# A modulation row summed on TensorE in two bursts, the row before it released later

## The chip, the core and the metric

The kernel runs on one core of a Trainium2 chip. The metric is the device time of one execution in microseconds (us), as the median of several runs. Five engines work side by side: TensorE (PE, matrix products; its weight loads are listed as PEld), VectorE (DVE), ScalarE (ACT), GpSimd (POOL) and SyncE (SP, which here only issues transfers). Each engine takes its own instructions in the order in which the program wrote them. An engine waits when an operand is not there, or when a buffer that it is to write is still being read.

## What is computed

Two transformer layers in a row over 256 positions of width 1024, in float32. The change lies in the second layer, which begins with six modulation rows:

```
mod = silu(c) @ mod_w + mod_b          # c: one row of 1024; mod_w: 1024 x 6144
shift1, scale1, gate1, shift2, scale2, gate2 = split(mod, 6)
h = rms_norm(x) * (1 + scale1) + shift1
(sc_b, sc_c, sc_x, q, k, v, z, xbc, dt_raw, gl_a, gl_b, gl_c) = split_columns(h @ w_in)
y_a = short_conv_mixer(sc_b, sc_c, sc_x) @ w_sc_out
y_b = stick_breaking_attention(q, k, v) @ w_sb_out
y_c = mamba2_mixer(z, xbc, dt_raw) @ w_ssm_out
merged = sigmoid(gl_a) * y_a + sigmoid(gl_b) * y_b + sigmoid(gl_c) * y_c
x = x + gate1 * rms_norm(merged @ w_o)
h2 = rms_norm(x) * (1 + scale2) + shift2      # then a gated FFN, gate2, residual
```

The rows are numbered g = 0 to 5 in the order shift1, scale1, gate1, shift2, scale2, gate2. Rows 3 and 4 (shift2, scale2) are read only after `w_o`.

## The kernel before

**Projections.** Every float32 product is made of three passes in a rounded format: each weight tile of 128 x 1024 is loaded by SP into `wst` (4 buffers), rounded by ACT into `wh` (L202), and DVE forms the rest `wl` (L203). PE then multiplies `x3h` with `wh`, `x3h` with `wl` and `x3l` with `wh` (L377, L379, L381, in rows of four matmuls of 256 columns). A *unit* is two such weight tiles, 12 rows of four matmuls, into one PSUM bank. SP can load a tile only when L203 has freed a `wst` buffer.

**The mixer of the second layer.** Its units come in the order that `mix2_order` gives: `qk0`, `qk1`, `xbc1`, `xbc0`, `xbc2` (the state-space channels, in three pairs), `sc1`, `sc0`, `sc2` (the short convolution), and then the gates `gl` of three branches, each with an output projection that writes `mg`. An `xbc` unit is followed by a convolution over the positions: ACT makes the first tap (L660), DVE the other three (L664), ACT a tanh, and a last DVE instruction sets the flag `xbc0`, `xbc1` or `xbc2`. Units, scores and bursts draw their PSUM banks from one pool of four, in turn: a unit cannot begin before the unit four places ahead of it in that pool has been read.

**Work beside it.** Whatever is not a projection is written as a generator in the list `chains`. `beside()` gives every chain one step; it is called twice for each weight tile, so after every three rows of four matmuls. `pause(name)` waits as many steps as the table `LAG` says, `need(flag)` waits until a flag is set, and `hold(1)` and `held` count PSUM banks. Two large chains run here: `stick_steps`, the attention (scores `z3`; ACT L1689 to L1691; DVE L1693, L1695; PE L1700 to L1704; DVE L1708; ACT L1710, L1712; PE L1719) and `ssm_steps`, the state-space scan (DVE L1622, L1623; ACT L1624; DVE L1634; PE L1671 to L1673).

**Modulation rows.** `mod_steps` makes one row after the other. A row needs 8 tiles `raw` of 128 x 1024 (512 KB each), which POOL loads ahead into 4 buffers. There are two ways to sum a row:

- for rows in `BY_SUMS`, DVE multiplies each tile by its scalar and adds it into `macc` (L1404, then L1406), one tile a step; 3 idle steps later four matmuls against ones (L1394) sum over the partitions;
- for the others, PE does it all: one step is a *burst* of 16 matmuls (L1394), four tiles times four column groups of 32 PE columns, into one bank.

After each sum DVE adds the bank to the row (L1396); POOL then writes the finished row out (L1425) and reads it back onto all partitions (L1426). Before the change, rows 0, 1 and 4 are in `BY_SUMS`. The first two and a half rows are done before the mixer; the second burst of row 3 and all of row 4 (12 steps) are the chain `mods_beside`, whose steps are separated by the pauses `mod` (2) and `mod2` (7). The chain sets the flag `mods`, for which the kernel waits ahead of `w_o`. Row 5 is done later, beside `w_o` and the FFN.

Of the kernel before, what the change touches and what calls it, by code (L numbers as in the profile page):

```python
# [19 lines left out]
KT = 8  # L20
# [9 lines left out]
for _n, _w in (("mlcw", 32), ("mlcb", 8), ("fcw", 132), ("fcb", 44), ("sccw", 6), ("ssmcw", 24),  # L30
# [33 lines left out]
WST = 4  # L64
WSP = 6

BY_SUMS = (0, 1, 4)

IDLE = 3

# [62 lines left out]
def block_pair(ctx, tc, a, out):  # L133
# [203 lines left out]
    chains, holders, heldA = [], [], [0]  # L337
# [9 lines left out]
    def need(*keys):  # L347
        while not flags.issuperset(keys):
            yield
# [110 lines left out]
    def drain(gen, n=None):  # L460
        if n is None:
            for _ in gen:
                pass
        else:
            for _ in range(n):
                next(gen, None)
# [258 lines left out]
    def pause(name, d=2):  # L725
        for _ in range(LAG[name]):
            yield


    held = [0]  # L730

    def hold(n):
        while held[0] + n > 4:
            yield
        held[0] += n
# [645 lines left out]
    def mod_steps():  # L1381
# [3 lines left out]
        for g in range(6):  # L1385
# [11 lines left out]

            if g in BY_SUMS:

# [32 lines left out]
    def mod_step(n=1):  # L1432
        drain(steps, n)
# [292 lines left out]

    def mods_beside(n):
        for i in range(n):
            mod_step()
            yield from pause("mod" if i < KT else "mod2")  # L1730
        flags.add("mods")

    chains.append(mods_beside(KT + IDLE + 2))

    def unit2(name, srcs, *stages):
        unit(name, srcs, xb, *stages, wide=False)
# [289 lines left out]
```

## Time and profile before

| | |
|---|---|
| median of 3 runs | 853.41 us (846.42 to 855.21) |
| the profiled execution | 853.56 us, of which the span from first to last instruction is 851.6 us |
| PE busy | 822.2 us (97%) |
| DVE busy | 601.4 us (71%) |
| ACT busy | 424.6 us (50%) |
| mixer of the second layer | from 452 to about 620 us |

PE is the engine that bounds the kernel: outside its first microseconds it rarely waits. So the time is read from where PE waits, from the clock that it is granted, and from what is put into its queue.

### The profile page before, as it was taken

The page shows a single profiled execution, that of the slowest core. Times are in us where ns is not written, and L with a number is a line of the kernel's source. Part 1 is how long each engine was busy: PE and PEld are TensorE (multiplying, and loading weights), DVE is VectorE, ACT ScalarE, POOL GpSimd, SP SyncE. Part 2 cuts the span into 40 slices and gives each one's busy share as a digit, 9 for nine tenths or more (in the row PEclk, how much of TensorE's full clock was granted, in tenths as well). Part 3 has the DMA queues.
Part 4 walks back from the last instruction along what each step waited for, and adds up shares of the span by engine and source line. Part 5 has one row for each costly group of instructions (what it writes and reads, how often), then busy time and mean ns, then how long its engine had stood idle before and what let it go on. Part 6 is the DMA issues. An engine that isn't in the chain of part 4 may idle for free.

```text
span 851.6 us, 14309 instructions
## 1 busy us (share of the span) xinstructions
PE 822.2 (97%) x5628; PEld 744.7 (87%) x5628; DVE 601.4 (71%) x1001; ACT 424.6 (50%) x633; POOL 64.6 (8%) x112
## 2 busy tenths in 40 slices
PE   6999999999999999999989999999999999999996
PEld 6999887998789998999769887999987799999994
DVE  4698688765748899887775987577579575554434
ACT  5655654455437567555343556454454464444421
POOL 1000200100010001000121210003110000000000
PEclk9999999999999999999999989999999999999999
DMA  7854774473445898886479964446666287556601
GB/s 263 311 162 139 259 249 152 136 255 99 150 148 178 283 325 269 332 266 210 138 286 383 347 228 149 144 142 193 184 222 252 78 257 249 188 183 188 190 33 49
DMA packets 50866, 176.03 MB, mean 207 GB/s; under 512 B 5900, under 2 KB 7088, under 8 KB 50800
## 3 DMA queue, kind: packets, MB, share of 16 engines
q1 hardware_dynamic: 40352, 138.64, 48.8%
q0 software_dynamic: 10448, 36.48, 12.5%
q8 instruction: 44, 0.72, 0.3%
q14 instruction: 22, 0.18, 0.1%
HBM read 174.02 MB, written 1.09 MB: 206 GB/s over the span
## 4 chain that ended last, share of the span: by engine, by line
PE 65%; DVE 9%; DMA 4%; ACT 3%; issue 2%; POOL 0%; DVEq 0%; ACTq 0%
PE pb L377 12%; PE pb L379 12%; PE pb L381 12%; PE pa L387 6%; PE pa L389 6%; PE pa L388 6%; PE pa L1248 3%; DVE wl L203 3%; ACT wh L202 1%; DMA wst<-in_w_xbc 1%; PE pa L381 1%; PE pa L379 1%; PE pa L377 1%; DMA wst<-in_w_sc 1%; PE pb L1180 1%
## 5 line engine op out<-in xcount | busy, mean ns | idle before, releaser
L203 DVE TENSOR_TENSOR wl<-wst,wh 128x1024 fp32r<-128x1024 f32 (+3 forms) x257 | 311.6, 1224 | 154.7 <-ACT wh L202 153.7
L202 ACT CAST wh<-wst 128x1024 fp32r<-128x1024 f32 (+3 forms) x257 | 263.8, 1037 | 242.8 <-PE pb L381 97.5
L387 PE MATMUL pa<-wh,hh 128*128 128x512 f32 x176 | 69.2, 393 | 0.7 <-ACT hh L202 0.7
L388 PE MATMUL pa<-wl,hh 128*128 128x512 f32 x176 | 69.3, 394 | 0.4 <-DVE wl L203 0.4
L389 PE MATMUL pa<-wh,hl 128*128 128x512 f32 x176 | 69.2, 393 | 0.0
L377 PE MATMUL pb<-x3h,wh 128*128 128x256 f32 x320 | 53.0, 288 | 1.9 <-DVE cv L664 1.9
L381 PE MATMUL pb<-x3l,wh 128*128 128x256 f32 x320 | 51.8, 285 | 0.0
L379 PE MATMUL pb<-x3h,wl 128*128 128x256 f32 x320 | 51.8, 284 | 0.0
L664 DVE SCALAR_TENSOR_TENSOR cv<-pb,sm,cv 128x255 f32<-128x255 f32 (+2 forms) x106 | 43.5, 474 | 11.6 <-ACT cv L660 11.6
L377 PEld LDWEIGHTS pb<-x3h,wh 128*128 128x128 f32 x320 | 44.7, 195 | 2.9 <-ACT lk L1691 2.1
L377 PE MATMUL pb<-x2h,wh 128*128 128x256 f32 x288 | 46.2, 282 | 0.0
L379 PE MATMUL pb<-x2h,wl 128*128 128x256 f32 x288 | 46.0, 282 | 0.0
L377 PE MATMUL pb<-x4h,wh 128*128 128x256 f32 x288 | 46.0, 282 | 0.0
L379 PE MATMUL pb<-x4h,wl 128*128 128x256 f32 x288 | 46.0, 282 | 0.0
L381 PE MATMUL pb<-x4l,wh 128*128 128x256 f32 x288 | 46.0, 282 | 0.0
L381 PE MATMUL pb<-x2l,wh 128*128 128x256 f32 x288 | 45.9, 282 | 0.0
L381 PEld LDWEIGHTS pb<-x3l,wh 128*128 128x128 f32 x320 | 44.6, 194 | 0.0
L379 PEld LDWEIGHTS pb<-x3h,wl 128*128 128x128 f32 x320 | 44.5, 193 | 0.0
L209 POOL DMA_DIRECT2D raw<-in_mod_w x48 | 25.3, 531 | 250.9 <-DVE macc L1406 97.0
L377 PEld LDWEIGHTS pb<-x2h,wh 128*128 128x128 f32 x288 | 39.7, 190 | 1.3 <-ACT wh L202 0.4
L377 PEld LDWEIGHTS pb<-x4h,wh 128*128 128x128 f32 x288 | 39.9, 190 | 0.7
L387 PEld LDWEIGHTS pa<-wh,hh 128*128 128x128 f32 x176 | 33.1, 188 | 7.8 <-ACT hh L202 1.1
(433 smaller groups left out, 1637.6 us busy)
## 6 DMA issues: line engine op xcount, KB each, us to landing
raw<-in_mod_w POOLq DMA_DIRECT2D x48, 512.0 KB, 6.7
wst<-in_ffn_up SPq DMA_DIRECT2D x44, 512.0 KB, 5.1
wst<-in_ffn_in SPq DMA_DIRECT2D x44, 512.0 KB, 4.2
wst<-in_w_gl SPq DMA_DIRECT2D x24, 512.0 KB, 3.7
wst<-in_ffn_down SPq DMA_DIRECT2D x22, 512.0 KB, 4.9
wst<-in_ffn_out SPq DMA_DIRECT2D x22, 512.0 KB, 3.6
wst<-in_w_qk SPq DMA_DIRECT2D x12, 512.0 KB, 6.7
wst<-in_xk SPq DMA_DIRECT2D x8, 512.0 KB, 4.0
```

Of the source, the lines that this page charges most:

```text
L202: A.copy(xh, src)
L203: V.tensor_tensor(xl, src, xh.bitcast(F32), ALU.subtract)
L209: (queue or nc.sync).dma_start(st[:, :n].rearrange("p (a b) -> p a b", a=src.shape[1]), src)
L377: T.matmul(dst, wh[:, k - k0, c0:c0 + P], xh[:, k, t0:t1], start=(k == ks[0]), stop=False)
L379: T.matmul(dst, wl[:, k - k0, c0:c0 + P], xh[:, k, t0:t1], start=False, stop=False)
L381: T.matmul(dst, wh[:, k - k0, c0:c0 + P], xl[:, k, t0:t1], start=False, stop=(k == ks[-1]))
L387: T.matmul(dst[:, c0:c1], xh[:, k, tsl], wh[:, kw, c0:c1], start=first, stop=False)
L388: T.matmul(dst[:, c0:c1], xh[:, k, tsl], wl[:, kw, c0:c1], start=False, stop=False)
L389: T.matmul(dst[:, c0:c1], xl[:, k, tsl], wh[:, kw, c0:c1], start=False, stop=last)
L664: V.scalar_tensor_tensor(dst[:, j:S], ps[:, 0:S - j], taps[K - 1 - j], dst[:, j:S], ALU.mult, ALU.add)
L1180: T.matmul(pl[:, tt * S:(tt + 1) * S], qx[:, 2 * h + e, tt * P:(tt + 1) * P], kx[:, 2 * h + e, :], start=(e == 0), stop=(e == 1))
L1248: T.matmul(pt, x_[:, 2 * i + kw, tsl], w_[:, kw, :], start=(i + n + kw == 0), stop=(i + n + kw == 6))
```

## The change

Row 4 leaves `BY_SUMS`, so it is summed by PE in two bursts. `mods_beside` has now three steps: the second burst of row 3, and the two of row 4. None of them is made until the flag `xbc0` is set (the second pair of state-space channels to be convolved), and 16 steps lie between one and the next.

```diff
-    "ml.4": 0, "ml.5": 1, "ml.s0": 4, "ml.s1": 7, "ml.s2": 9, "ml.s3": 4, "mod": 2, "mod2": 7, "no.0": 0, "no.1": 0, "no.2": 1,
+    "ml.4": 0, "ml.5": 1, "ml.s0": 4, "ml.s1": 7, "ml.s2": 9, "ml.s3": 4, "mod2": 16, "no.0": 0, "no.1": 0, "no.2": 1,
...
-BY_SUMS = (0, 1, 4)
+BY_SUMS = (0, 1)
...
     def mods_beside(n):
         for i in range(n):
+            yield from need("xbc0")
+            yield from hold(1)
             mod_step()
-            yield from pause("mod" if i < KT else "mod2")
+            held[0] -= 1
+            yield from pause("mod2")
         flags.add("mods")

-    chains.append(mods_beside(KT + IDLE + 2))
+    chains.append(mods_beside(3))
```

Three places show what moves. The first is DVE between the projections `qk` and the convolution of the first state-space pair (`xbc1`, whose taps are the three rows L664). Before:

```order
L203 TENSOR_TENSOR wl_5090<-wst_4933,wh_5089 128x1024
L1406 SCALAR_TENSOR_TENSOR macc_4949<-raw_4951,cs,macc_4949 128x1024
L203 TENSOR_TENSOR wl_5124<-wst_4989,wh_5123 128x1024
L1406 SCALAR_TENSOR_TENSOR macc_4949<-raw_5005,cs,macc_4949 128x1024
L203 TENSOR_TENSOR wl_5171<-wst_5023,wh_5170 128x1024
L1406 SCALAR_TENSOR_TENSOR macc_4949<-raw_5038,cs,macc_4949 128x1024
L664 SCALAR_TENSOR_TENSOR cv_5058<-pb_5060,sm,cv_5058 128x255 x2
L664 SCALAR_TENSOR_TENSOR cv_5058<-pb_5060,sm,cv_5058 128x254 x2
L664 SCALAR_TENSOR_TENSOR cv_5058<-pb_5060,sm,cv_5058 128x253 x2
```

The same place with the change:

```order
L203 TENSOR_TENSOR wl_5045<-wst_4903,wh_5044 128x1024
L203 TENSOR_TENSOR wl_5076<-wst_4953,wh_5075 128x1024
L203 TENSOR_TENSOR wl_5120<-wst_4984,wh_5119 128x1024
L664 SCALAR_TENSOR_TENSOR cv_5016<-pb_5018,sm,cv_5016 128x255 x2
L664 SCALAR_TENSOR_TENSOR cv_5016<-pb_5018,sm,cv_5016 128x254 x2
L664 SCALAR_TENSOR_TENSOR cv_5016<-pb_5018,sm,cv_5016 128x253 x2
```

All eight instructions on `macc` are gone from DVE, and with them the transfers of `raw` that each of them let go.

The second place is PE between the end of the attention's second score product (L1704) and the first outputs of the scan (L1671, which read `ar`). Before:

```order
L1703 MATMUL pa_5540<-qb,kb 128x128
L1704 MATMUL pa_5540<-lk_5586,ntri 128x128
L1394 MATMUL pb_5665<-macc_4949,triu 32x256 x4
L1671 MATMUL pa_5676<-xdt,ar_5638 128x64
L1672 MATMUL pa_5676<-xdt,ar_5638 128x64
```

With the change:

```order
L1703 MATMUL pa_5513<-qb,kb 128x128
L1704 MATMUL pa_5513<-lk_5559,ntri 128x128
L1394 MATMUL pb_5635<-raw_5383,cs 32x256 x4
L1394 MATMUL pb_5635<-raw_5385,cs 32x256 x4
L1394 MATMUL pb_5635<-raw_5387,cs 32x256 x4
L1394 MATMUL pb_5635<-raw_5389,cs 32x256 x4
L1671 MATMUL pa_5666<-xdt,ar_5611 128x64
L1672 MATMUL pa_5666<-xdt,ar_5611 128x64
```

The four matmuls that closed row 4 before are replaced at this very place by its first burst of 16. The row's second burst stands later, within the third `gl` unit; row 3's second burst has moved from the middle of `qk0` to the middle of `sc0`.

The third place is DVE at the same moment: L1708 masks the attention's scores, L1634 makes the `ar` that L1671 reads, L1396 empties the burst's bank. Before:

```order
L1623 SCALAR_TENSOR_TENSOR ar_5642<-aq_5276,acs,maskn 128x128
L1708 TENSOR_TENSOR att_5660<-pa_5540,maskn 128x2x128 x2
L1634 TENSOR_TENSOR ar_5638<-gm_5636,ar_5638 128x384
L1634 TENSOR_TENSOR ar_5642<-gm_5636,ar_5642 128x384
L1396 TENSOR_TENSOR brow_4947<-pb_5665,brow_4947 128x256
```

With the change:

```order
L1623 SCALAR_TENSOR_TENSOR ar_5615<-aq_5219,acs,maskn 128x128
L1396 TENSOR_TENSOR brow_5633<-pb_5635,brow_5633 128x256
L1708 TENSOR_TENSOR att_5661<-pa_5513,maskn 128x2x128 x2
L1634 TENSOR_TENSOR ar_5611<-gm_5609,ar_5611 128x384
L1634 TENSOR_TENSOR ar_5615<-gm_5609,ar_5615 128x384
```

L1396, which reads what the burst leaves, now stands ahead of L1708 and of both L1634.

## Rows read from the trace of the kernel before

**Rows 1.** PE's waits, 452 to 610 us: total us, times, longest.

```profile
PE pa L1700 <- DVE lk L1693: 2.0, 2, 1.1
PE pb L377 <- DVE cv L664: 1.9, 1, 1.9
PE pa L1671 <- DVE ar L1634: 0.7, 1, 0.7
```

**Rows 2.** Timeline of PE: start us, us, engine, line, operation, count [idle before <-releaser].

```profile
487.38 0.71 PE L377 MATMUL pb<-x3h,wh 128*128 128x256 f32 x4 [1.89 <-DVE cv L664]
...
491.42 0.70 PE L1700 MATMUL pa<-qb,kb 64*128 64x256 f32 x2 [0.92 <-DVE lk L1693]
...
493.72 1.12 PE L1700 MATMUL pa<-qb,kb 64*128 64x256 f32 x2
...
497.51 1.20 PE L377 MATMUL pb<-x3h,wh 128*128 128x256 f32 x4
```

**Rows 3.** Stretches of 4 us: PE busy (count), granted clock, DMA share, GB/s.

```profile
484.00:488.00 4.00, 2.11 (x18) 1.00 1.03 409
...
492.00:496.00 4.00, 4.00 (x15) 0.73 0.79 262
496.00:500.00 4.00, 4.00 (x17) 0.50 0.59 184
500.00:504.00 4.00, 4.00 (x32) 0.91 0.73 247
```

**Rows 4.** Timeline of ACT and DVE, 478 to 492 us.

```profile
478.82 1.05 ACT L202 CAST wh<-wst 128x1024 fp32r<-128x1024 f32 x1 [6.28 <-DMA wst<-in_w_sc]
...
481.40 1.05 ACT L202 CAST wh<-wst 128x1024 fp32r<-128x1024 f32 x1 [1.53 <-DMA wst<-in_w_sc]
482.36 1.02 ACT L660 ACTIVATE cv<-pb,sm 128x256 f32<-128x256 f32 x2
...
484.82 2.42 DVE L664 SCALAR_TENSOR_TENSOR cv<-pb,sm,cv 128x255 f32<-128x255 f32 x6
...
490.41 0.95 DVE L1693 SCALAR_TENSOR_TENSOR lk<-pa,lk 128x768 f32<-128x768 f32 x1
```

**Rows 5.** DVE's groups on `macc`, 466 to 490 us: busy us, mean ns of one.

```profile
L1406 DVE SCALAR_TENSOR_TENSOR macc<-raw,cs,macc 128x1024 f32<-128x1024 f32 x7 | 8.9, 1278 | 0.0
...
L1404 DVE TENSOR_SCALAR macc<-raw,cs 128x1024 f32<-128x1024 f32 x1 | 0.8, 751 | 0.0
```

**Rows 6.** DMA issues, 440 to 540 us: count, size, median us to landing.

```profile
raw<-in_mod_w POOLq DMA_DIRECT2D x16, 512.0 KB, 8.0
wst<-in_w_gl SPq DMA_DIRECT2D x10, 512.0 KB, 3.7
wst<-in_w_sc SPq DMA_DIRECT2D x8, 512.0 KB, 7.4
```

**Rows 7.** Timeline of PE: a burst in `qk0`, and what follows it.

```profile
453.65 1.93 PE L1394 MATMUL pb<-raw,cs 128*32 128x256 f32 x32
455.52 0.74 PE L377 MATMUL pb<-x3h,wh 128*128 128x256 f32 x4
```

**Rows 8.** Timeline of PE and DVE at the end of row 4.

```profile
528.75 0.64 PE L1394 MATMUL pb<-macc,triu 128*32 128x256 f32 x8
528.86 0.75 DVE L1708 TENSOR_TENSOR att<-pa,maskn 128x256 f32<-128x256 f32 x2 [1.53 <-PE pa L1704]
529.53 1.02 DVE L1634 TENSOR_TENSOR ar<-gm,ar 128x384 f32<-128x384 f32 x2
...
530.13 0.43 PE L1671 MATMUL pa<-xdt,ar 128*128 128x64 f32 x2 [0.74 <-DVE ar L1634]
```

**Rows 9.** Timeline at a burst of row 5, for which DVE waits.

```profile
665.21 1.93 PE L1394 MATMUL pb<-raw,cs 128*32 128x256 f32 x32
...
667.21 0.42 DVE L1396 TENSOR_TENSOR brow<-pb,brow 128x256 f32<-128x256 f32 x1 [0.58 <-PE pb L1394]
```

**Rows 10.** Timeline of PE ahead of the mixer: a long single wait.

```profile
439.87 1.29 PE L480 MATMUL pb<-ident,h__729_4638 128*128 128x128 f32 x8 [2.49 <-DVE h__729_4638 L1472]
```

## The prediction

> **What bounds the kernel now.** I read three views in this order: PE's waits in the mixer, the clock granted there, and what DVE, ACT and the DMA queues do ahead of the waits. PE is the bound: from 452 to 610 us it waits for only 4.6 us in all [rows 1]. So a change pays here only through those waits and the clock, and costs whatever PE work it adds.
>
> Two of the waits stand close together: 1.89 us before unit `sc1`, whose bank DVE has not yet emptied of `xbc1`, and 0.92 us before the attention's second scores [rows 2]. Shortly after them the granted clock falls to half, 1.2 instead of 2.4 GHz: 0.73, 0.50 and 0.91 of full speed over three stretches of 4 us in which PE is busy throughout [rows 3]. That costs 4 x (0.27 + 0.50 + 0.09) = 3.4 us. The place loses 1.89 + 0.92 + 3.4 = 6.2 us altogether. PE had worked without a break until the first of the two waits, so I take the fall to be their result.
>
> Why do they arise? The convolution of `xbc1` on DVE (L664) begins at 484.82 and ends 2.42 us later, just when PE can go on; its first tap on ACT (L660) came at 482.36, behind two roundings of weights that had waited 6.28 and 1.53 us for their transfers [rows 4]. The transfers are late because DMA is full: a share of 1.03 at 409 GB/s [rows 3], with sixteen tiles `raw` landing after 8.0 us and `w_sc` after 7.4 us, where `w_gl`, mostly later, needs 3.7 us [rows 6]. DVE meanwhile spends 8.9 + 0.8 = 9.7 us on `macc` [rows 5].
>
> **The change part by part.**
>
> *DVE's sums leave.* Eight instructions, 9.7 us of DVE [rows 5], stood between the weights' L203 and the convolution. With them go the transfers of `raw` that they released one at a time; and since row 3's second burst now waits for `xbc0`, no new `raw` is loaded until then. If `w_sc` lands like `w_gl`, 3.7 us earlier [rows 6], ACT's two waits (7.8 us) shrink by about half or more: I estimate that L660 comes 4 to 5 us earlier, and DVE, with no `macc` ahead, makes L664 at about 478 to 479. PE reaches `sc1` at 485.49 (487.38 less the wait) in this trace, and 1.87 us sooner without the burst in `qk0`, at 483.6. DVE is then done with a margin of some 2 us. The wait at L1700 depends on L1693 (490.41 [rows 4]), which lies behind ACT's chain and one more L1406; 5 us and 1.28 us earlier it ends near 485, and PE is there at 486.5. Both waits go: -2.8 us. PE works without a break there, so the clock has no cause to fall: -3.4 us. Bounds: nothing (if other work keeps DVE late) to -6.2 us. I take -6.2, because two causes are removed and either covers the 1.89 us.
>
> *Row 3's second burst moves* from `qk0` to the middle of `sc0`. A burst holds PE for 455.52 - 453.65 = 1.87 us [rows 7], as much in one place as in the other: 0. Its four tiles landed long before. Its L1396 (0.42 us) stands ahead of an L203 for weights that PE needs a unit half later; that and the 1.87 us that PE itself loses there cover it. Uncovered it would cost 0.4 us.
>
> *Row 4's first burst* takes the place of the four `macc` matmuls at 528.75. On PE that is 1.87 us instead of 0.64. But the wait is more: before, DVE did L1708 and L1634 while PE ran these matmuls, and L1671 began at 530.13, 0.74 us late, at once after the first L1634 [rows 8]. Now L1396 stands ahead of L1708. DVE sits there until the burst has ended, at 528.75 + 1.93 = 530.68, and begins 0.07 us later (as 667.21 stands to 665.21 + 1.93 [rows 9]). L1708 follows after some 0.4 us, and from the start of L1708 to that of L1671 it took 530.13 - 528.86 = 1.27 us [rows 8]. L1671 begins at 530.75 + 0.4 + 1.27 = 532.4: 2.3 us later than before, of which PE idles 1.75 us. Bounds: 1.87 - 0.64 = 1.2 us, if nothing stood in DVE's queue, to 2.3. DVE's order is fixed, so 2.3. L1710, L1712 and L1719 come later by no more than that. Its tiles are let go by the burst 16 steps before.
>
> *Row 4's second burst* lies within a `gl` unit, where PE waits for nothing: +1.87 us. The L1396 behind it holds DVE for a moment; nothing of PE depends on it before four more banks have been drawn.
>
> *POOL's queue.* The last of the scan's transfers (L1628) now stands behind four `raw` that wait for row 4's first burst. They are released at 530.7 and take about 2 us to issue, so it issues at 533, where before it stood behind L1426. No cost. Row 5's tiles are loaded after the last burst, before `w_o`.
>
> Without the clock: 853.56 - 6.2 + 2.3 + 1.87 = 851.5 us, against the profiled 853.56, which stands 0.15 us from the median of 853.41.
>
> *The clock, again.* The wait of 1.75 us at 530.7 lies in a long run of plain float32 matmuls: L1591, L1700 to L1704, the burst, L1671, L1719. The other wait of this kind, at most 1.1 us for L1693 [rows 1], stands 7 us ahead of it and stays, for its chain on ACT keeps step with PE. Before, 0.74 us and these together left the clock alone; at 493 us, 2.81 us in two pieces, the second before L1700 to L1704, did not [rows 2, 3]. The new pair comes to 2.8 us, with no dense projection between them. That is nearest to the row at which the clock fell. I take one low stretch of the same size, 3.4 us, with bounds 0 and 6.8. The Trainium skill (TensorE: Matmul & The Clock Gate, "What's actually happening") has the clock gated when the engine has lately been idle, which would name the longest single wait as the risk. The trace does not bear that out: a single wait of 2.49 us at 437 us [rows 10] left the clock at full speed, and shorter ones beside float32 work cost it. The page's section "A second HAM failure mode" speaks of many small idles between groups that throttle the clock, which fits this place better. By the first the sum is 851.5 us, by the second 854.9.
>
> **Forecast.** 851.5 + 3.4 = 854.9 us: the gain at 485 us is given back at 529 us and after. I give it 0.43.
>
> **The rivals.**
>
> - *The clock holds* at the new wait, as it did at the 2.49 us [rows 10] and at the 0.74 us of before [rows 8]. 851.5 us. Chance 0.29.
> - *A long low stretch* (the slower side). The clock falls already at the first of the two waits, at 523, and stays at half through the float32 run until dense units have worked again. At half speed a score group took 497.5 - 493.7 instead of 493.7 - 491.4 us [rows 2], about 1.5 us more; two groups, the burst, the outputs and a dense tail come to 6.5 to 7 us: 858.3 us. Against it: before, this run kept full clock with its own 1.8 us of waits. It would be slower by over 1% only from 10.4 us lost, a low stretch of 21 us. Chance 0.12.
> - *The change does not free PE at 485 us.* DVE and ACT stay late for reasons of their own, the clock falls there, and the bursts are added: 853.56 + 4.2 = 857.7 us. Against it: ACT's late start is the transfers'. Chance 0.09.
> - *The waits at 523 and 530 go too*, because a DVE with less to do is ahead: 851.5 - 1.75 - 1.1 = 848.7 us, and less if other waits follow. Against it: both are tied to PE's own results. Chance 0.07.
>
> **How the numbers follow.** The likeliest gives 854.9 us. The range runs from 849.5 (the clock holds and some 2 us of waits go as well) to 858.4 us (the long low stretch and the unfreed PE); the likeliest alone would have 853 to 857. A measurement of this kernel can tell about 1% from no change: the runs before spread over that much. Faster by over 1% is below 844.9, which no case reaches without something unseen: 0.04. Slower by over 1% is above 861.9: the tail of the two slow cases, 0.05. Within 1%: 0.91.
>
> **What would show it.** Right: PE without a wait between 480 and 500 us and at full clock there; `w_sc` landing in about 4 us; three bursts of 1.9 us after 490 us; a wait of about 1.75 us for L1634 before L1671, released behind L1396; and a stretch at half clock within 10 us of it. Wrong: waits for L664 or L1693 before 500 us (then DVE or ACT was late without `macc`); L1671 without a wait (then L1396 did not hold DVE); full clock throughout (then the time is near 851.5).

## The result, and the profile after

| | before | after |
|---|---|---|
| median beside one another on one chip, 20 executions each | 854.21 us (844.76 to 860.25) | 856.88 us (853.59 to 860.61) |
| the profiled execution | 853.56 us, span 851.6 us | 858.92 us, span 857.0 us |
| ratio of after to before | | 1.0057, 95% interval 1.0037 to 1.0077 |

The change makes the kernel 0.6% slower: less than 1%, but its interval leaves out 1. The ratio compares the executions and is not that of the two medians, which lie 2.7 us apart; the means (852.7 and 857.0 us) lie 4.3 us apart. The forecast was 854.9 us, the measured median is 856.88, within the range that was given (849.5 to 858.4). But the change itself was forecast at 854.9 - 853.56 = 1.3 us, and by the ratio it is 0.0057 x 854 = 4.9 us. So the time came out near; the steps behind it were not all right, and errors cancelled in part.

PE's waits of after, 440 to 620 us (total us, times, longest), which answer to [rows 1] and [rows 10]:

```profile
PE pa L1671 <- DVE ar L1634: 3.4, 1, 3.4
PE pb L480 <- DVE h__729_4638 L1472: 2.7, 1, 2.7
PE pa L1700 <- DVE lk L1693: 1.1, 1, 1.1
```

The waits for L664 and for the first L1693 are gone; the wait at L1671 has grown from 0.7 to 3.4 us. Now the stretches of 10 us of after: busy time (count) of PE, PEld, DVE, ACT and POOL, then the granted clock, the DMA share and GB/s, as in [rows 3]:

```profile
480.00:490.00 10.00, 10.00 (x73) 8.79 (x71) 7.94 (x17) 7.73 (x10) 0.54 (x1) 1.00 0.47 152
490.00:500.00 10.00, 10.00 (x95) 8.65 (x95) 8.13 (x15) 6.23 (x11) 2.78 (x6) 1.00 0.72 216
...
520.00:530.00 10.00, 6.57 (x55) 4.46 (x54) 4.81 (x13) 3.22 (x8) 3.18 (x6) 0.92 0.76 251
530.00:540.00 10.00, 10.00 (x50) 8.77 (x50) 1.73 (x4) 0.86 (x2) 0.54 (x1) 0.56 0.30 114
```

From 480 to 500 us PE works throughout at full clock, as forecast. From 528.5 to 539 us it works at half clock: 10 x (0.08 + 0.44) = 5.2 us lost.

The transfers went as the sum said (DMA issues of after, 440 to 540 us: count, size, median us to landing; compare [rows 6]), and ACT's first tap came at 477.22 (timeline; 482.36 in [rows 4]):

```profile
wst<-in_w_gl SPq DMA_DIRECT2D x10, 512.0 KB, 3.6
wst<-in_w_sc SPq DMA_DIRECT2D x8, 512.0 KB, 4.2
...
477.22 1.02 ACT L660 ACTIVATE cv<-pb,sm 128x256 f32<-128x256 f32 x2
```

The place that was mis-sized is row 4's first burst. Timeline of after, 522 to 529 us (start us, us, engine, line, operation, count [idle before <-releaser]), which answers to [rows 8]:

```profile
522.21 0.54 POOL L1628 DMA_DIRECT2D aq<-d  x1 [3.56 <-DVE ar L1623]
522.74 0.54 POOL L1387 DMA_DIRECT2D brow<-in_mod_rows  x1
523.34 1.93 PE L1394 MATMUL pb<-raw,cs 128*32 128x256 f32 x32
527.10 0.42 DVE L1396 TENSOR_TENSOR brow<-pb,brow 128x256 f32<-128x256 f32 x1 [5.19 <-DMA brow<-in_mod_rows]
527.44 0.75 DVE L1708 TENSOR_TENSOR att<-pa,maskn 128x256 f32<-128x256 f32 x2
528.11 1.02 DVE L1634 TENSOR_TENSOR ar<-gm,ar 128x384 f32<-128x384 f32 x2
528.71 0.69 PE L1671 MATMUL pa<-xdt,ar 128*128 128x64 f32 x2 [3.43 <-DVE ar L1634]
```

The burst ends at 525.27, and L1396 could begin then. It begins at 527.10, because its other operand, the tile `brow` with the row's bias and gain, is not there. The same step of the chain that issues the burst issues that tile's load (L1387), on POOL, one instruction behind a load of the scan (L1628) that waits 3.56 us for DVE. From L1387 to L1396 pass 4.36 us. Behind L1396 stand L1708 and L1634, and PE waits for L1634 for 3.43 us.

### The profile page after: what moved, and what is told of

It reads as the page before. It is cut to its first block, busy times and chain, and to the rows that moved or that the text cites. A ratio compares the mean times of both kernels' runs of the same rounds, so it can differ in the third digit from the quotient of the medians.

```text
span 857.0 us, 14409 instructions
## 1 busy us (share of the span) xinstructions
PE 828.3 (97%) x5684; PEld 749.2 (87%) x5684; DVE 593.3 (69%) x994; ACT 425.1 (50%) x633; POOL 64.7 (8%) x112
## 4 chain that ended last, share of the span: by engine, by line
PE 73%; DVE 7%; ACT 2%; issue 1%; DMA 1%; DVEq 0%; POOL 0%; ACTq 0%
PE pb L377 13%; PE pb L379 13%; PE pb L381 13%; PE pa L387 7%; PE pa L388 7%; PE pa L389 7%; PE pa L1248 3%; DVE wl L203 1%; PE pb L1394 1%; PE pa L381 1%; PE pa L379 1%; PE pa L377 1%; PE pb L1180 1%; PE pb L1206 1%; PE pb L480 1%
## 5 line engine op out<-in xcount | busy, mean ns | idle before, releaser
L664 DVE SCALAR_TENSOR_TENSOR cv<-pb,sm,cv 128x255 f32<-128x255 f32 (+2 forms) x106 | 43.5, 473 | 11.6 <-ACT cv L660 11.6
```

The costliest lines, as they stand in the source:

```text
L664: V.scalar_tensor_tensor(dst[:, j:S], ps[:, 0:S - j], taps[K - 1 - j], dst[:, j:S], ALU.mult, ALU.add)
```

## The experiments

Each kernel is timed beside the kernel before on the same chip. The first number is the median; the ratio is to before over the executions, with its 95% interval.

**One theory, two halves.** The theory after reading the two traces: L1671's wait has two parts, L1396 standing ahead of L1634 on DVE (the 1.75 us that the sum had) and the bias tile being late (the rest, 1.7 us), and the wait brings the low clock behind it. Rival: the bursts' own PE work is the excess, or the bursts bring the low clock whatever DVE does. The first kernel loads row 4's bias tile a burst earlier, at the end of row 3 (L1679 here is L1671, L1642 is L1634):

```diff
+    early4 = []
...
-            bt = mp.tile([P, 2, 256], F32, tag="brow", name=nm("brow"))
-            G.dma_start(bt, a["mod_rows"][g])
+            if g == 4:
+                bt = early4[0]
+            else:
+                bt = mp.tile([P, 2, 256], F32, tag="brow", name=nm("brow"))
+                G.dma_start(bt, a["mod_rows"][g])
...
             G.dma_start(mods[g], d.rearrange("a b -> (a b)").unsqueeze(0).to_broadcast([P, D]))
+            if g == 3:
+                early4.append(mp.tile([P, 2, 256], F32, tag="brow", name=nm("brow")))
+                G.dma_start(early4[0], a["mod_rows"][4])
             yield
```

> The changed kernel, but row 4's own tile (bias and gain, the brow that L1396 adds to) is loaded at the end of row 3, some 20 us ahead, instead of in the step of the burst. Theory 'transfer': L1396 stood 5.19 us waiting for that tile, which POOL issued only after L1628; with the tile there, L1396 starts 0.07 us after the burst, and PE's wait before L1671 falls from 3.43 to the predicted 1.75 us. The time falls by 1.7 us for that alone, and by up to 3.4 us more if the low clock shortens from 10.2 us: 852 to 855 us. Rival 'burst': PE's burst of 32-column matmuls itself brings the clock down and L1634 is late for its own operands; then the wait stays above 3 us and the time at 856 to 857 us.

Measured: 853.11 us median, 1.004 (1.0007 to 1.0074). Its timeline:

```profile
527.07 0.43 PE L1679 MATMUL pa<-xdt,ar 128*128 128x64 f32 x2 [1.68 <-DVE ar L1642]
```

With the tile there the wait is 1.68 us, the 1.75 us of the sum. So the order on DVE was costed rightly, and the transfer was what it left out. The low clock did not shorten with the wait: in this execution there are stretches at half clock from 517.5 to 525 and from 528 to 535 us, the first of them ahead of L1671, for 6.8 us lost against 5.2 in after's.

The second kernel leaves the tile late and issues L1396 of that burst (L1399 here) three steps later, behind both L1634 (L1676 is L1671 here, L1639 is L1634, L1705 is L1700):

```diff
+    late_add = []
...
-                V.tensor_tensor(res, pm_[:, 0:256], res, ALU.add)
+                if g == 4 and not late_add:
+                    late_add.append(lambda: V.tensor_tensor(res, pm_[:, 0:256], res, ALU.add))
+                    return
+                V.tensor_tensor(res, pm_[:, 0:256], res, ALU.add)
...
             mod_step()
+            if i == 1:
+                for _ in range(3):
+                    yield
+                late_add[0]()
...
-            yield from pause("mod2")
+            for _ in range(LAG["mod2"] - 3 * (i == 1)):
+                yield
```

> The changed kernel, but the add L1396 of row 4's first burst is put three steps later, behind L1708 and both L1634 on DVE; PE's queue is as in the changed kernel. Theory 'DVE order': L1634 is done while PE runs the burst, PE's wait before L1671 goes from 3.43 us to about 0, and without it the clock holds there: 3.4 + up to 5.1 us less, 849 to 852 us in the median. Rival 'burst': the wait goes but the low stretch after the burst stays: 853 to 854 us. If the wait stays, it was not DVE's order.

Measured: 849.7 us, 0.998 (0.9949 to 1.0011). PE's waits from 440 to 620 us, the timeline at that L1396, and two stretches:

```profile
PE pa L1705 <- DVE lk L1698: 1.1, 1, 1.1
PE pb L381 <- DVE sparel L1805: 0.8, 1, 0.8
...
526.01 0.42 DVE L1399 TENSOR_TENSOR brow<-pb,brow 128x256 f32<-128x256 f32 x1 [2.36 <-DMA brow<-in_mod_rows]
...
520.00:530.00 10.00, 9.18 (x83) 6.92 (x82) 4.80 (x13) 3.88 (x9) 3.70 (x7) 1.00 0.88 290
530.00:540.00 10.00, 10.00 (x86) 10.00 (x86) 5.39 (x10) 4.20 (x8) 0.00 (x0) 1.00 0.42 133
```

The burst is at the same place, DVE still waits 2.36 us for the bias tile, but PE does not wait at the scan's outputs, and in this execution the clock stays up from 510 to 540 us.

**Other places for the bursts.** One kernel puts 24 steps between them, so that none stands between the attention's scores and L1671:

```diff
-"mod2": 16
+"mod2": 24
```

> The changed kernel with 24 steps between the bursts instead of 16, so that row 4's two bursts lie within dense gl units; the same instructions, no burst between L1704 and L1671. Theory 'DVE order': L1671 waits about 1.2 to 1.3 us (the time of L1708 and one L1634, before 0.74 us behind four matmuls), the clock holds as before the change did there, each burst costs its 1.87 us: about 850 to 851 us. Rival 'burst': a low stretch follows a burst wherever it stands: 853 to 855 us.

Measured: 858.82 us, 1.0095 (1.0057 to 1.0133), where both theories had 850 to 855 us. PE's waits from 440 to 620 us and the stretches:

```profile
PE pb L377 <- ACT gs L1814: 2.3, 1, 2.3
PE pa L1671 <- DVE ar L1634: 1.3, 1, 1.3
...
510.00:520.00 10.00, 8.92 (x42) 6.69 (x41) 6.50 (x11) 6.20 (x9) 1.08 (x2) 0.78 0.60 195
520.00:530.00 10.00, 8.69 (x33) 6.55 (x32) 3.60 (x9) 2.04 (x5) 1.06 (x2) 0.50 0.24 79
```

The waits at the scan are as small as expected, but the clock is low from 515.5 to 533 us, with no burst between 500 and 536 us. So a burst is not what starts a low stretch there. A new wait of 2.3 us, with 1.7 us lost to the clock from 594 us on, goes with the later burst: POOL's adds into `mg` stand behind the row's read-back, which waited 9.0 us.

Another does not wait for `xbc0`, and makes the bursts in `qk0`, `qk1` and `xbc1`:

```diff
-            yield from need("xbc0")
-            yield from hold(1)
             mod_step()
-            held[0] -= 1
-            yield from pause("mod2")
+            for _ in range(6 if i < 2 else 16):
+                yield
```

> The row is summed in bursts as in the changed kernel, but the bursts do not wait for xbc0: they stand in qk0, qk1 and xbc1, six steps apart, so the raw tiles are loaded between 454 and 475 us again, while DVE has no macc. It tells which of the two causes made PE wait at 485 and 491 us before. Theory 'DVE' (macc delayed the convolution): no wait for L664 or L1693, no low clock near 494, time about 850.5 us. Theory 'DMA' (raw delayed w_sc and with it ACT's L660): ACT's waits for w_sc stay near 8 us, PE waits over 1 us at sc1 and the clock falls there: 854 to 857 us.

Measured: 864.31 us, 1.0145 (1.0103 to 1.0187). PE waits for the bursts' tiles, 440 to 620 us:

```profile
PE pb L1394 <- DMA raw<-in_mod_w: 6.1, 5, 1.9
```

Neither theory had this: the bursts themselves came to wait for the full DMA (a share of 0.82 to 1.03 from 450 to 490 us). PE waits neither for L664 nor at the first L1700, but it comes there later by its own waits. Holding the bursts until `xbc0` avoids these waits.

**What held the convolution at 485 us.** Two kernels are made from the kernel before. The first leaves row 4's transfers out and keeps DVE's sums, the second keeps the transfers and shrinks the sums:

```diff
-            raws[g, k] = fetch(mp, "raw", 4, a["mod_w"][g, k].rearrange("p (a b) -> p a b", a=4), G)
+            if g == 4:
+                raws[g, k] = mods[2]
+            else:
+                raws[g, k] = fetch(mp, "raw", 4, a["mod_w"][g, k].rearrange("p (a b) -> p a b", a=4), G)
```

> The kernel before, with row 4's eight multiply-adds kept on DVE in their places, but its eight transfers left out: they read a tile that lies ready (so row 4 of the modulation is wrong), and row 5's first four tiles are loaded after row 4. Theory A (transfers): the waits at 485 to 492 us come of the full DMA. Then w_sc lands in about 4 us (7.4 before), ACT's waits for it come to about 4 us (7.8), L660 starts 4 to 5 us earlier, and both of PE's waits (1.89 and 0.92 us) and the low clock behind them go although DVE still makes its 9.7 us of sums: about 847 us profiled, ratio 0.993. Theory B (DVE): the sums themselves hold the convolution back; L664 is still late, PE waits 1 us or more for it, and the time stays near 853.

```diff
-                        V.scalar_tensor_tensor(macc, st, cs[:, k:k + 1], macc, ALU.mult, ALU.add)
+                        n = 64 if g == 4 else D
+                        V.scalar_tensor_tensor(macc[:, 0:n], st[:, 0:n], cs[:, k:k + 1], macc[:, 0:n], ALU.mult, ALU.add)
```

> The kernel before, with all of row 4's transfers kept, but its seven multiply-adds on 64 columns instead of 1024 (so the other columns of row 4 are wrong): DVE has some 8 us less, DMA the same. Theory A (transfers): w_sc still lands in 7 us or more, ACT waits 7 to 8 us for it, L660 comes at about 482, and PE still waits, some 0.5 to 1.9 us, for L664. Theory B (DVE): the wait for L664 goes, and the low clock with it: about 847. If both this and the kernel without transfers free PE, either cause alone was enough, as the prediction said.

Measured: 852.65 us, 0.9985 (0.9951 to 1.002), and 853.1 us, 1.0008 (0.9972 to 1.0045). Without transfers, `w_sc`'s landing, ACT's first tap and DVE's taps:

```profile
wst<-in_w_sc SPq DMA_DIRECT2D x8, 512.0 KB, 4.1
...
477.80 1.02 ACT L660 ACTIVATE cv<-pb,sm 128x256 f32<-128x256 f32 x2
...
482.99 2.42 DVE L664 SCALAR_TENSOR_TENSOR cv<-pb,sm,cv 128x255 f32<-128x255 f32 x6
```

With the sums shrunk:

```profile
wst<-in_w_sc SPq DMA_DIRECT2D x8, 512.0 KB, 7.5
...
480.62 1.02 ACT L660 ACTIVATE cv<-pb,sm 128x256 f32<-128x256 f32 x2
...
482.08 2.42 DVE L664 SCALAR_TENSOR_TENSOR cv<-pb,sm,cv 128x255 f32<-128x255 f32 x6
```

In the first, ACT is 4.6 us earlier than in [rows 4] and DVE's sums hold L664 back to 482.99; in the second ACT is only 1.7 us earlier, but DVE is free. Either way L664 begins 1.8 to 2.7 us earlier, and both waits of PE at 485 to 492 us are gone. That either removal alone is enough, as the prediction said, is not shown, though. In both of these executions PE had lost time at half clock before it came here, at the wait at L480 that [rows 10] shows (3.4 and 1.7 us lost, at 437 to 444 us), so PE itself came later; and before, unchanged, lacks the wait for L664 too in an execution with such a stretch (its second, below). Without transfers L664 ends at 485.41, and PE begins `sc1` only 0.2 us later:

```profile
440.00:450.00 10.00, 10.00 (x67) 6.91 (x67) 3.73 (x5) 4.47 (x5) 4.10 (x9) 0.80 0.62 224
...
485.60 0.67 PE L377 MATMUL pb<-x3h,wh 128*128 128x256 f32 x4
```

And the 6.2 us did not come: both medians are those of before. The trace without transfers has its loss further back:

```profile
490.00:500.00 10.00, 10.00 (x73) 9.01 (x73) 10.00 (x21) 5.02 (x8) 1.63 (x3) 1.00 0.58 183
...
520.00:530.00 10.00, 9.70 (x37) 6.64 (x35) 5.33 (x16) 3.56 (x9) 1.12 (x2) 0.50 0.31 90
530.00:540.00 10.00, 10.00 (x59) 8.78 (x59) 1.25 (x2) 1.39 (x2) 3.18 (x6) 0.69 0.74 276
```

Full clock at 490 us, but half clock from 519 to 536.5 us, 8.5 us lost, in code that was left alone. The profiled execution of the other kernel has no low stretch there and took 847.35 us, about the 847 that was expected; but eight of its ten executions took 851 to 855 us.

**The delay alone.** Row 4 summed by DVE as before, with its chain held until `xbc0`, 4 steps apart:

```diff
+        yield from need("xbc0")
         for i in range(n):
             mod_step()
-            yield from pause("mod" if i < KT else "mod2")
+            for _ in range(4):
+                yield
```

> The kernel before (row 4 by DVE's sums), with its chain held until xbc0 as in the change, and 4 steps between one step and the next: the delay alone, without the bursts of row 4. If the delay is what frees PE at 485 us, then there is no wait between 480 and 515 us as in the kernel after, and the bursts' price is not paid: L1671 waits 0 to 1 us, the profile gives 853.6 - 6.2 = 847.4 us plus at most one low stretch of 3 to 5 us. If the bursts were needed, because DVE's sums are in the way wherever they stand, PE waits for L1634, L1693 or L664 come to 2 us or more after 500 us, and the time is 850 to 855.

Measured: 855.76 us, 1.0055 (1.0032 to 1.0079): the rival, 0.8 us above its range. PE's waits, 430 to 640 us:

```profile
PE pb L1660 <- DVE sparel L203: 2.7, 1, 2.7
PE pa L1671 <- DVE ar L1634: 2.1, 1, 2.1
```

The front is free of waits here too, but DVE's sums now stand ahead of the scan's instructions, and cost there what the bursts cost.

**The same kernels again.** Since taking away the waits at 485 us left the median where it was, before and after were profiled again, unchanged.

> The kernel before, unchanged, a second profiled execution. The profile that the prediction rested on had a mean granted clock of 0.994, while most runs of before had 0.983 to 0.988, and taking row 4's transfers or DVE's sums away removed the waits at 485 to 492 us without a change of the median. Theory A: the 3.4 us of low clock at 493 to 500 us belong to that execution, not to the program; a common execution (clock near 0.988, 852 to 854 us) has its low stretch elsewhere, 13 to 17 us long, most likely from about 519 us on, where the attention's second scores wait 1.1 us. Theory B: the waits of 2.8 us at 485 to 492 us and the low stretch behind them recur here, as the prediction assumed, with another stretch beside them.

> The kernel before, unchanged, a third profiled execution. Theory A: the same waits (within 0.5 us each) but a low stretch at another place or of another length than in the first two by 3 us or more. Theory B: waits and low stretch at 485 to 500 us as in the first.

> The kernel after, unchanged, a second profiled execution: which of its low-clock stretches belong to the program and which to the execution. If the wait at L1671 (3.4 us) causes the stretch behind it, wait and stretch (528 to 539 us, 10 us long) recur at the same place. If the stretch depends on the execution, it is missing, or begins elsewhere or ends at another time by 3 us or more, with the same waits.

Measured: 852.19, 858.42 and 854.19 us, one execution each. The second execution of before has no wait for L664, a full clock at 490 us, and low stretches at 438 to 442 us (1.7 us lost) and at 520 to 534 us (6.8 us lost):

```profile
PE pa L1700 <- DVE lk L1693: 1.7, 2, 1.1
...
490.00:500.00 10.00, 10.00 (x77) 9.32 (x76) 10.00 (x21) 5.92 (x10) 1.62 (x3) 1.00 0.71 213
...
520.00:530.00 10.00, 9.70 (x38) 6.72 (x39) 4.99 (x13) 4.07 (x9) 2.22 (x4) 0.51 0.24 81
```

The third has both, the wait for L664 with the low stretch behind it, and a longer one from 522.5 to 540 us (8.5 us lost):

```profile
PE pb L377 <- DVE cv L664: 1.6, 1, 1.6
...
490.00:500.00 10.00, 10.00 (x45) 8.17 (x44) 10.00 (x21) 3.50 (x5) 1.62 (x3) 0.66 0.69 224
...
520.00:530.00 10.00, 8.91 (x27) 5.93 (x26) 5.42 (x11) 4.75 (x7) 1.07 (x2) 0.64 0.46 157
530.00:540.00 10.00, 9.70 (x46) 7.51 (x46) 4.37 (x11) 2.04 (x5) 1.69 (x3) 0.50 0.24 80
```

So both theories were half right. The front's wait for L664 and low stretch came in two of three executions, and the stretch from about 520 us in two of three as well: the one execution that the sum was made against was the one without it. In after's second execution the wait recurs (3.16 us) with a low stretch of 3.4 us lost instead of 5.2.

**Projections between the small products.** L1700 to L1719 stand in one run without projections, because the short convolution's output projection waits for `scu` to be split. Two pauses of 2 steps instead of 7 and 6 split it earlier and put rows of projections between the scores and L1671 (in after 6 ahead of the burst and 12 behind it; in before all of them ahead of row 4's L1394):

```diff
-    "sc2.1": 7, "sc2.2": 6,
+    "sc2.1": 2, "sc2.2": 2,
```

> The kernel before, with one thing changed: the short convolution's product is split 9 steps earlier (pauses sc2.1 and sc2.2 of 2 instead of 7 and 6), so its projection is not kept waiting while the chains are stepped alone; L1700 to L1704, row 4's L1394, L1671 and L1719, which stood in one run of some 10 us, now have dense projections between them. Theory A (a run without projections, with waits in it, is what costs the clock): no low stretch from 510 to 550 us, the mean clock of the common execution rises from 0.988 to 0.994 or more, waits of L1700 and L1671 below 1 us together, median 845 to 848, ratio 0.992 to 0.995. Rival (the clock falls somewhere in any case): the median stays at 851 to 854 with its low stretch at another place, or the projection waits 1 to 3 us for the split itself.

> The kernel after with that one thing changed. There are now projections (6 rows) between the attention's scores and row 4's first burst, and 12 rows between the burst and L1671. Theory A: L1671 does not wait (3.4 us in after), though its bias tile still comes as late and L1396 still stands ahead of L1634; no low stretch from 515 to 550 us; median 856.9 - 3.4 - 1 - about 5 = 847 to 849, ratio 0.993 to 0.996. Rival: DVE, held by L1396 for the bias tile, makes PE wait 2 us or more at the next bank or weight instead, or the clock falls elsewhere: 852 to 857.

Measured: 857.82 us, 1.0092 (1.0055 to 1.0128), and 858.1 us, 1.0086 (1.005 to 1.0123). PE's waits of the second, 430 to 660 us, and a stretch:

```profile
PE pb L381 <- DVE sparel L1795: 3.0, 1, 3.0
PE pb L377 <- ACT spareh L202: 2.2, 1, 2.2
...
510.00:520.00 10.00, 7.05 (x48) 6.54 (x47) 7.29 (x13) 6.34 (x9) 1.50 (x3) 0.90 0.64 201
```

Neither L1700 nor L1671 waits any more, but the split itself is late by 3.0 us, and a low stretch stands behind that wait and behind the 2.2 us one (1.7 us lost at each). So a run without projections is not needed for a low stretch: wait and low stretch moved. The first of the two, which has before's front, waits 2.2 us for L664 at 485 us, with 1.7 us lost behind it.

**The mended versions beside after.**

> The kernel after, unchanged, timed beside the kernel before and the two mended versions on the same chip. Theory (the wait at L1671 and the low clock behind it are the whole excess): median 855 to 858, ratio to before 1.003 to 1.008, in the profile a wait of 3.2 to 3.4 us at L1671 with half clock behind it. Rival (the excess is the bursts' own PE work): the mended versions beside it come to within 2 us of it.

> The kernel after with row 4's first L1396 three steps later, behind both L1634, as run once before (849.7 us median). Theory: no wait for L1634 and at most one low stretch before 452 us in the profile; 6 to 8 us below after in the median, 849 to 851. If its first result was luck of the executions, the median comes to 853 or more and the profile shows a low stretch at 515 to 540 us without a wait at L1671.

> The late L1396 and the bias tile of row 4 loaded a burst earlier, together. If the place of L1396 alone decides, this is the same as the late L1396 alone within 1 us (849 to 851), since nothing waits for the bias tile there. If the late bias tile still costs something further back, by holding DVE at the late L1396, this one is 1 to 2 us faster.

Measured: after 855.91 us, 1.0066 (1.0039 to 1.0093); the late L1396 again 849.77 us, 0.9987 (0.9955 to 1.0019); late L1396 and early tile together 852.72 us, 1.0001 (0.9971 to 1.0032). The late L1396 repeats its 849.7 us and is 6 us below after, though five of its 24 executions took 854 to 856 us. The two changes together were expected equal to it and came out 3 us higher in the median, and no row explains it: its profiled execution was free of low stretches from 430 to 620 us, six of its twelve executions took 847 to 852 us and six 854 to 855. That one is inconclusive. After's third execution shows the wait at L1671 in another size:

```profile
527.24 3.64 PE L1394 MATMUL pb<-raw,cs 128*32 128x256 f32 x32
530.95 0.42 DVE L1396 TENSOR_TENSOR brow<-pb,brow 128x256 f32<-128x256 f32 x1 [8.03 <-PE pb L1394]
...
532.55 0.43 PE L1671 MATMUL pa<-xdt,ar 128*128 128x64 f32 x2 [1.67 <-DVE ar L1634]
```

Here the clock fell before the burst, which took 3.64 us at half speed; the bias tile landed meanwhile, L1396 waited for the burst, and the wait is again the 1.7 us of DVE's order.

## Why the prediction came out as it did

Two terms of the sum were mis-sized. Row 4's first burst was put at 2.3 us and cost 4.0 in the execution that was shown first, because a transfer was left out. The place at 485 us was put at 6.2 us from one execution, and brought 3.9 on average. The low stretch behind the new wait was put at 3.4 us, and before turned out to have one there in two of its three traces. What follows is the evidence for each.

To compare kernels over all executions whose clock is on record, I split each into the span at full clock (span times mean granted clock, an estimate) and what the clock took (the rest of the span). The median is of the times, the other two columns are means:

| kernel | executions | median us | at full clock, us | lost to the clock, us |
|---|---|---|---|---|
| before | 98 | 852.3 | 841.2 | 8.3 |
| after | 33 | 856.5 | 845.5 | 9.5 |
| early bias tile | 12 | 853.1 | 844.6 | 8.4 |
| late L1396 | 24 | 849.7 | 844.0 | 4.6 |
| both | 12 | 852.7 | 842.3 | 7.6 |

The profiled execution of before lost 851.6 x 0.006 = 5.1 us to the clock, below the mean of 8.3. Before's executions are of two kinds: 33 of the 98 took less than 850 us, and most of the rest 851 to 856. After has none of the first kind; its lowest is 853.59. The last column is no price by itself: every trace ends at half clock, 1.4 to 3.0 us of it, but from row 5's second burst to the end all six traces of before and after take the same 186.4 to 186.5 us.

The three traces of each kernel can also be cut at places that both have: the end of the wait at L480 (439.87 in [rows 10]), the second pair of scores, and row 5's second burst (665.21 in [rows 9]). In the first trace of before the scores stand at 524.13 us, in that of after the two places at 518.72 and 670.58 us (the first line is before's):

```profile
524.13 0.70 PE L1700 MATMUL pa<-qb,kb 64*128 64x256 f32 x2 [1.08 <-DVE lk L1693]
...
518.72 0.70 PE L1700 MATMUL pa<-qb,kb 64*128 64x256 f32 x2 [1.09 <-DVE lk L1693]
...
670.58 1.93 PE L1394 MATMUL pb<-raw,cs 128*32 128x256 f32 x32
```

| three executions each, in order, us (of it lost to the clock) | before | after | change of the mean |
|---|---|---|---|
| L480 to the scores | 84.3 (3.4), 79.6 (1.7), 84.1 (3.4) | 78.7 (1.7), 77.5 (0), 80.1 (3.4) | -3.9, forecast -6.2 |
| the scores to row 5's second burst | 141.1 (0), 146.3 (6.8), 147.8 (8.5) | 151.9 (5.1), 150.2 (3.4), 152.4 (8.5) | +6.4, forecast 2.3 + 1.87 + 3.4 = +7.6 |

Three executions are an indication and no more. Of the +6.4 us, 5.8 are not the clock's (forecast 4.2, so 1.6 more) and 0.6 are (forecast 3.4).

- **The waits at 485 and 491 us** go: right, in all three executions of after, one of them without a low stretch ahead of the place. L664 began at 478.49 in the first (forecast 478 to 479). Removing both causes does it; that either alone would is not shown.
- **Their worth, 6.2 us**: wrong for the median. The wait for L664 stood in two of three executions of before, and in the third PE came later by a low stretch at 438 us instead; the two kernels with one cause removed kept the median of before within about 0.5%. This step read one execution as the program.
- **Row 3's moved burst** at 0, and **row 4's second burst** at 1.87 us: PE waits for neither of them in after's list of waits. Nothing contradicts the terms.
- **Row 4's first burst, 2.3 us with a wait of 1.75**: the step that failed in its mechanism. The order on DVE was right (1.68 us with the tile there, 1.67 in after's third execution). The sentence "Its tiles are let go by the burst 16 steps before" thought of `raw` alone; `brow` is issued by the same step as the burst, behind L1628 on POOL. The wait was 3.43 us (3.16 in the second execution), so the term was 1.7 us short.
- **One low stretch of 3.4 us behind the new wait**: it came, with 5.2 us (3.4 in the other two executions). That the wait causes it is not shown. The two kernels in which L1671 does not wait are 5.1 and 6.4 us below after by the means, more than the wait of 1.7 to 3.4 us itself. How that splits is not settled: with the late L1396 alone it is 1.5 us of the span at full clock and 4.9 us of the clock, with both changes 3.2 and 1.9. And the stretch is not all new: before lost 6.8 and 8.5 us at the same place in two of its three executions, so the prediction's premise that the waits of before left the clock alone there held for one execution. Against these the clock's part of the change is 9.5 - 8.3 = 1.2 us by the means, and not 3.4.
- **The rivals.** "The clock holds" came in none of after's three traces; the late L1396, whose clock held at this place in both traces, has no such wait. "A long low stretch" from the first wait on happened in after's third execution (520.5 to 531 us), and in before itself.

By the profiled executions: 853.56 - 6.2 + 2.3 + 1.7 + 1.87 + 5.2 = 858.4 us, and 858.92 was measured; after's execution also has a low stretch of 1.7 us lost at 439.5 us, in code that the change leaves alone, which that sum lacks. Over the executions the gain of 6.2 is smaller, the burst dearer, and the clock's part of the loss smaller. That these errors partly cancel, so that the time fell into the range, is luck.

What stays open: what decides whether the clock falls at the 1.1 us wait for L1693, which all traces of before and after have and only some pay for; whether the wait at L1671 brings a low stretch that would not have come otherwise; and how a before execution of 847 us looks, since none was profiled (the nearest is the kernel with the sums shrunk, at 847.35 us without a low stretch between 443 and 842 us). Of the two mended versions, the late L1396 has the lowest median of all kernels run, about 7 us below after, but its two intervals to before both include 1.

## What to carry to other kernels

When work moves to another engine, list every operand of the instruction that receives its result, with the queue that issues each: a 256 KB bias tile behind one blocked load on POOL doubled, in two of three executions, a wait that was costed rightly without it. An instruction that collects a result should be issued behind the instructions that the bound engine waits for next; moving this one three steps took 5 to 6 us off (the two versions that do it, by the means). And before a stretch of low clock is entered in a sum, look at more than one execution: its place and length change between executions of one kernel.

## What the runs showed of the hardware

- **Low-clock stretches move between executions of the same program.** Before had them at 493.5 to 501, at 520 to 534, and at 492 to 499 with 522.5 to 540 us. The first and the third have the same waits there within 0.5 us, and the third lost 8.5 us more. The Trainium skill (TensorE: Matmul & The Clock Gate, "What's actually happening") says that the same kernel can start with a different number of slow matmuls from run to run; these traces show such a difference in the middle of a kernel too.
- **At one place the clock fell only behind the longer waits.** The Trainium skill (the same page and section) has the clock set by how busy the engine has been recently; the prediction set that aside, because a wait of 2.49 us ahead of the mixer left the clock at full speed [rows 10]. At that place, the wait for L1472 (L480 on PE), the seventeen traces of this study show more: in six the wait was 1.72 to 2.49 us, and none has a low stretch behind it; in eleven it was 2.64 to 2.99 us, and eight have one, as after itself (2.7 us in its list of waits):

```profile
440.00:450.00 10.00, 10.00 (x72) 7.59 (x73) 3.11 (x5) 5.06 (x6) 4.11 (x9) 0.84 0.63 212
```

  After's second execution, with 2.98 us, has none. So one row had been taken for a rule. Whether the wait of 3.43 us at L1671 was a risk by its length alone is not shown.
- **Low stretches can last far longer than the waits at them.** In the kernel with bursts 24 steps apart, half clock held from 515.5 to 533 us, with PE busy for 8.9 and 8.7 of 10 us, after a wait of 1.1 us and with one of 1.3 us within; in the two kernels with the early split, waits of 2.2 and 3.0 us among projections were each followed by 1.7 us lost.
- **A slower PE hides waits.** At half clock the burst took 3.64 us instead of 1.93, and the wait behind it fell from 3.43 to 1.67 us. Before's front shows the same: the wait for L664 stands in the three traces whose clock held at 440 us (1.6 to 2.2 us) and is missing in before's second, where it fell, as in the two kernels with one cause removed, where it fell too. So clock losses and waits can't be added up from different executions.
